# A hybrid attention block on one core: the causal mask added by TensorE, and a norm weight loaded as one row

## The chip, the core and the metric

The kernel runs on one core of a Trainium2 chip. The core has five engines that run side by side and wait for each other through semaphores: TensorE (PE in the profile; its weight loads are shown apart as PEld), VectorE (DVE), ScalarE (ACT), GpSimd (POOL) and SyncE (SP), which here issues all the transfers between HBM and the on-chip memory. Products are written to PSUM, which has 8 banks of 128 partitions by 512 fp32 numbers. The metric is the time of one execution on the device in microseconds (us), lower is better.

## What is computed

One layer of a streaming encoder on 1024 positions of width 1024, all in fp32:

```python
h = rms_norm(x, norm_pre_g)
proj = h @ w_in                          # -> sb_q, sb_k, sb_v, sb_g, c_q, c_kv, k_rope, mla_g
# group A: 8 stick-breaking heads; past = key < query (strictly)
log_fail = where(past, log_sigmoid(-z), 0); suffix = cumsum from the right
w = where(past, exp(log_sigmoid(z) + suffix), 0);  sb_o = w @ v
# group B: 8 latent-attention heads, chunk mask, softmax
y = concat(norm(sb_o) * silu(sb_g), norm(mla_o) * silu(mla_g)) @ w_out
x = x + rms_norm(y, norm_post_g)
x = x + rms_norm(p @ w_ple) * sigmoid(x @ w_ple_gate + b)
```

## The kernel before, in words

**Recorder and scheduler.** The program is not issued as it is written. A recorder takes down every operation, and a list scheduler (`schedule`, line 313) then decides the order on each engine from a table of costs and latencies, a priority per operation (its place in the code plus a bias, `R.bias`) and the buffers that are free. `issue` (line 482) issues the operations in that order; for that reason every row of the profile has the line L514. Tile names in rows: `u` and `f` are two pools of 512 KB buffers in SBUF, `t` are five PSUM banks (transposes and scores), `a` three PSUM banks (products that accumulate), `h` four large SBUF buffers (first the normed input, later the output weights), `ident` the identity for transposes.

**Precision.** For the large products every fp32 operand is split into a high part, which TensorE multiplies in one pass (type fp32r), and a low remainder (`split`: a cast, on ACT or DVE, and a subtraction, on DVE or POOL as the table `SPLITS` says); three products of the parts replace one. Transposes are products with the identity in fp32.

**Head.** `HEAD` orders the first transfers: a quarter of the v weights (`v0`), token tiles 1 and 0 of x, the vector norm_pre_g (`g0`), then the other quarters and x tiles. The vector is loaded by a transfer that reads its 4 KB 128 times and writes 512 KB, the same row on each partition (`bcast`, line 614). `x_norm` (line 639) squares a tile on ACT, takes the root on POOL and multiplies tile, root and vector in one DVE operation; `x_tr` (line 652) transposes the 128x1024 tile in two groups of four and splits the result; then the projections begin.

**Attention.** 16 head pairs (`SEQ`: head pair c, half s; c under 4 is stick-breaking, c from 4 on latent attention; s=0 is the first 512 queries, s=1 the second) are worked through one unit (one head, one half) after the other, in rows of 128 queries. `sb_rows` (line 1030) makes one stick-breaking row: two products into one or two PSUM banks, an addition of `maskt` (-1e30 on and above the diagonal) by DVE on the last 128 columns, two sigmoids by ACT, one product by POOL, one scan by DVE, one more product by POOL. `mla_rows` makes a latent row: three products, a DVE memset in place of a mask, row maxima by DVE, exponentials by ACT. `av` transposes the rows, splits them (ACT and DVE) and multiplies them with v. Between the rows, other work (projections, gates, low-rank products, output weights, first output tiles: `FILL0`, then `wo` and `e1`) is woven in; `RATES` says how much of it each unit takes.

**Tail.** After attention, `TAIL` orders the output products (`o`), the last gate products (`e`) and their loads (`x`) of the eight token tiles.

Of the kernel before, what the change touches and what calls it, by code (L numbers as in the profile page):

```python
# [12 lines left out]
F32 = mybir.dt.float32  # L13
F32R = mybir.dt.float32r
I32 = mybir.dt.int32
BF16 = mybir.dt.bfloat16
# [38 lines left out]
TAIL = ("x0", "o4", "o5", "o6", "x1", "x2", "e4", "o7", "e1", "x3", "e3", "e6", "e0", "e5", "e2", "e7")  # L55
RATES = (4.264, 8.284, 4.735, 4.524, 3.1, 1.429, 0.789, 1.173, 1.977, 0.816, 0.4, 1.023, 0.46, 0.671, 0.339, 1.676)
EARLY = 4
LATER = 5
SEQ = ((0, 0), (1, 0), (6, 0), (4, 0), (7, 0), (2, 0), (5, 0), (0, 1), (3, 0), (2, 1), (4, 1), (3, 1), (5, 1), (7, 1), (1, 1), (6, 1))
FILL0 = ("x4", "l0", "x5", "x6", "x7", "b1", "q1", "c0", "r3", "t0", "lrv0", "g3", "rope0", "r0", "g4", "r1", "q2", "r2", "q3", "g6", "g0", "g7", "g2", "g1", "ple0", "g5")  # L60
# [4 lines left out]
SPLITS = (1, 0, 1, 1, 0, 1, 1, 0, 1, 0, 1, 0, 1, 0, 0, 1, 1, 1, 1, 1, 1, 0, 1, 1, 1)  # L65
HEAD = ("v0", "x1", "x0", "g0", "v1", "v3", "v2", "x2")
# [93 lines left out]
class Recorder:  # L160
# [92 lines left out]
    def columns(self, op, args):  # L253

        return self.elems(args[0]) * (2 if op == "transpose" else 1 if args[1].dtype == F32R else 4)
# [8 lines left out]
    def cost(self, eng, op, args, kw, outs, aps, spaces):  # L264
        n = max(self.elems(a) for a in aps)
        ps = any(k == "psum" for _, k in spaces)
        if eng == "PE":
            n = self.elems(outs[0])
            if op == "transpose":
                return 109.0  # L270
            if aps[1].dtype == F32R:
                return n * 0.451 + 1 if n >= 256 else n * 1.67
# [244 lines left out]
def block_kernel(ctx, tc, x, p, positions, norm_pre_g, w_in, q_norm_g, w_uq, kv_norm_g, w_ukv,  # L517
# [44 lines left out]
    def small(tag, n=8, bufs=2):  # L562
# [5 lines left out]
    maskt = const([128, 128], "maskt")  # L568
    POOL.memset(maskt, 0.0)
    POOL.affine_select(maskt, maskt, pattern=[[-1, 128]], compare_op=ALU.is_gt, fill=NEG,  # L570
                       base=0, channel_multiplier=1)
    nhalf = const([128, 8], "nhalf")
# [66 lines left out]
    def x_norm(t):  # L639
# [6 lines left out]
        if t < EARLY:  # L646
            DVE.scalar_tensor_tensor(xt, xt, rs, gb["pre"], ALU.mult, ALU.mult)
# [67 lines left out]
    def first(item):  # L715
# [3 lines left out]
        elif k == "g":  # L719
            gb["pre"] = bcast(k4(dt=F32, name="gb_pre"), norm_pre_g, D)  # L720
# [35 lines left out]

    for item in HEAD:
        first(item)
    x_norm(0)
    x_norm(1)  # L760
    x_tr(0)
# [268 lines left out]
    def sb_rows(i, s, rows):  # L1030
        qa, qb, kk = stacks.pop((i, s))
        for qi in range(4):
# [5 lines left out]
            for ps, ks in tiles:  # L1038
                h = ks.stop - ks.start
                kw = slice(ks.start, ks.start + w)  # L1040
                mm(ps[:, 0:w], qa[:, qc], kk[:, kw], start=True, stop=False)
                mm(ps[:, 0:w], qb[:, qc], kk[:, kw], start=False, stop=True)
                if ks.stop == nk:
                    DVE.tensor_tensor(ps[:, h - 128:h], ps[:, h - 128:h], maskt, ALU.add)
# [377 lines left out]
```

## Time and profile before

| what | value |
|---|---|
| median of 3 runs (lowest to highest) | 795.59 us (793.53 to 798.85) |
| the profiled execution: its own time, its span | 796.6 us, 794.8 us |
| TensorE busy | 760.2 us (96%), 3880 products |
| VectorE busy | 544.2 us (68%) |
| ScalarE busy | 406.0 us (51%) |
| GpSimd busy | 344.1 us (43%) |
| share of the 16 transfer engines | 53.5% |

How to read it: busy time is the union of an engine's instructions. Products are pipelined and their ends are modelled, so short waits lie hidden in a busy TensorE. The program's own time is longer than the span by 1.8 us, which lie outside the instructions.

### The profile page before, as it was taken

The page shows a single profiled execution, that of the slowest core. Times are in us where ns is not written, and L with a number is a line of the kernel's source. Part 1 is how long each engine was busy: PE and PEld are TensorE (multiplying, and loading weights), DVE is VectorE, ACT ScalarE, POOL GpSimd, SP SyncE. Part 2 cuts the span into 40 slices and gives each one's busy share as a digit, 9 for nine tenths or more (in the row PEclk, how much of TensorE's full clock was granted, in tenths as well). Part 3 has the DMA queues.
Part 4 walks back from the last instruction along what each step waited for, and adds up shares of the span by engine and source line. Part 5 has one row for each costly group of instructions (what it writes and reads, how often), then busy time and mean ns, then how long its engine had stood idle before and what let it go on. Part 6 is the DMA issues. An engine that isn't in the chain of part 4 may idle for free. (4 is left out here: it accounts for less than half of the span.)

```text
span 794.8 us, 11668 instructions
## 1 busy us (share of the span) xinstructions
PE 760.2 (96%) x3880; PEld 629.5 (79%) x3880; DVE 544.2 (68%) x1063; ACT 406.0 (51%) x968; POOL 344.1 (43%) x321
## 2 busy tenths in 40 slices
PE   4999999999999999999998988999999999999997
PEld 3888889977888888788786767788888888788885
DVE  6866234399747796898788899999678897222222
ACT  5315123344436776766477878677966721121211
POOL 1836104102512270977980387233583183034342
PEclk9999999999999999999999999999999999999999
DMA  9554353187998576346754555867464364041321
GB/s 338 198 186 152 106 182 88 53 307 258 324 321 273 186 229 196 120 147 211 227 158 133 198 173 166 324 236 269 130 209 177 107 240 171 0 133 68 107 92 54
DMA packets 97308, 143.97 MB, mean 181 GB/s; under 512 B 7264, under 2 KB 54880, under 8 KB 97248
## 3 DMA queue, kind: packets, MB, share of 16 engines
q1 hardware_dynamic: 97248, 143.23, 53.5%
q8 instruction: 31, 0.51, 0.3%
q14 instruction: 29, 0.24, 0.1%
HBM read 96.54 MB, written 46.66 MB: 180 GB/s over the span
## 5 line engine op out<-in xcount | busy, mean ns | idle before, releaser
L514 POOL TENSOR_TENSOR u<-u,u 128x512 f32<-128x512 f32 (+17 forms) x168 | 234.9, 1411 | 202.9 <-ACT u L514 153.0
L514 PE MATMUL a<-h,f 128*128 128x512 f32 x864 | 238.1, 406 | 0.1
L514 PE MATMUL a<-u,u 128*128 128x512 f32 (+2 forms) x765 | 191.6, 377 | 0.3 <-DVE f L514 0.2
L514 PEld LDWEIGHTS a<-h,f 128*128 128x128 f32 x864 | 155.8, 189 | 28.7 <-DVE f L514 0.6
L514 DVE TENSOR_TENSOR u<-t,u 128x512 fp32r<-128x512 f32 (+4 forms) x280 | 147.2, 554 | 31.9 <-ACT u L514 25.3
L514 ACT CAST u<-t 128x512 fp32r<-128x512 f32 (+3 forms) x256 | 111.7, 488 | 97.7 <-PE t L514 74.5
L514 PEld LDWEIGHTS a<-u,u 128*128 128x128 f32 x765 | 138.1, 188 | 27.6 <-DVE u L514 0.9
L514 PE MATMUL t<-u,u 128*128 128x512 f32 (+4 forms) x588 | 147.5, 365 | 7.9 <-DVE u L514 4.6
L514 PE MATMUL t<-ident,u 128*128 128x128 f32 x792 | 131.5, 277 | 16.5 <-DVE u L514 13.5
L514 PEld LDWEIGHTS t<-u,u 128*128 128x128 f32 x588 | 101.5, 188 | 34.8 <-DVE u L514 10.3
L514 PEld LDWEIGHTS t<-ident,u 128*128 128x128 f32 x792 | 98.0, 142 | 37.1 <-DVE u L514 16.7
L514 ACT ACTIVATE u<-t 128x384 f32<-128x384 f32 (+5 forms) x208 | 92.7, 520 | 38.2 <-DVE t L514 22.2
L514 DVE TENSOR_TENSOR u<-a,u 64x512 f32<-64x512 f32 (+4 forms) x59 | 37.3, 641 | 75.4 <-PE a L514 63.4
L514 DVE TENSOR_TENSOR_SCAN u<-u 128x64 f32<-128x64 f32 (+3 forms) x64 | 63.8, 999 | 13.4 <-ACT u L514 13.0
L514 PE MATMUL a<-h,u 128*128 128x512 f32 x288 | 68.4, 396 | 1.4 <-DVE f L514 1.4
L514 ACT ACTIVATE f<-a 128x512 bf16<-128x512 f32 (+2 forms) x64 | 34.4, 539 | 67.2 <-PE a L514 52.6
L514 ACT ACTIVATE u<-t,nms 128x384 f32<-128x384 f32 (+4 forms) x96 | 55.1, 579 | 23.8 <-DVE nms L514 21.5
L514 PEld LDWEIGHTS a<-h,u 128*128 128x128 f32 x288 | 53.9, 188 | 14.5 <-DVE f L514 1.8
L514 DVE TENSOR_TENSOR f<-a,f 128x512 f32<-128x512 f32 (+2 forms) x54 | 34.4, 644 | 42.5 <-ACT f L514 41.1
L514 DVE TENSOR_REDUCE nm<-t 128x1 f32<-128x384 f32 (+4 forms) x96 | 51.9, 547 | 3.7 <-PE t L514 2.9
L514 PE MATMUL a<-u,h 128*128 128x512 f32 x192 | 49.1, 405 | 0.8 <-DVE h L514 0.8
L514 ACT ACTIVATE u<-u 128x512 f32<-128x512 f32 (+3 forms) x24 | 17.5, 739 | 51.6 <-DVE u L514 47.1
(90 smaller groups left out, 693.9 us busy)
## 6 DMA issues: line engine op xcount, KB each, us to landing
u<-q_d SPq DMA_DIRECT2D x64, 256.0 KB, 4.4
u<-k_d SPq DMA_DIRECT2D x16, 512.0 KB, 6.0
u<-v_d SPq DMA_DIRECT2D x16, 512.0 KB, 5.2
f<-in_w_in_dram SPq DMA_DIRECT2D x14, 512.0 KB, 5.7
v_d<-u SPq DMA_DIRECT2D x12, 512.0 KB, 3.9
f<-in_x_dram SPq DMA_DIRECT2D x9, 512.0 KB, 6.3
k_d<-u SPq DMA_DIRECT2D x9, 512.0 KB, 4.6
q_d<-u SPq DMA_DIRECT2D x9, 512.0 KB, 4.7
```

Source lines behind the costliest of these rows:

```text
L514: x["fn"](*[place(a) for a in x["args"]], **{k: place(a) for k, a in x["kw"].items()})
```

## The change

There are three edits and a new set of tables.

1. **The mask.** `maskt` becomes `mask`, of type bf16, and a bf16 identity `eye` is made beside it. The DVE addition goes; between a row's two score products stands a third that multiplies `eye` with `mask` and accumulates into the last 128 columns.
2. **The norm vector.** It is loaded as one row of 4 KB into one partition; two TensorE products with a row of ones spread each half of it over the 128 partitions, and two ACT copies bring it from PSUM to SBUF. These and the norm and transposes of tile 0 get priority (`URGENT`).
3. **Tile 0's norm** is made in two halves on DVE instead of one operation.
4. **Tables.** `SEQ`, `FILL0`, `RATES`, `SPLITS`, `TAIL` and `HEAD` have other entries.

```diff
-SEQ = ((0, 0), (1, 0), (6, 0), (4, 0), (7, 0), (2, 0), (5, 0), (0, 1), (3, 0), (2, 1), (4, 1), (3, 1), (5, 1), (7, 1), (1, 1), (6, 1))
+SEQ = ((0, 0), (1, 0), (6, 0), (4, 0), (7, 0), (2, 0), (0, 1), (3, 0), (3, 1), (2, 1), (5, 0), (5, 1), (7, 1), (4, 1), (1, 1), (6, 1))
-HEAD = ("v0", "x1", "x0", "g0", "v1", "v3", "v2", "x2")
+HEAD = ("v0", "x1", "x0", "g0", "v3", "v1", "v2", "x2")
+URGENT = 35
...
-    maskt = const([128, 128], "maskt")
-    POOL.memset(maskt, 0.0)
-    POOL.affine_select(maskt, maskt, pattern=[[-1, 128]], compare_op=ALU.is_gt, fill=NEG,
+    mask, eye = const([128, 128], "mask", BF16), const([128, 128], "eye", BF16)
+    POOL.memset(mask, 0.0)
+    POOL.affine_select(mask, mask, pattern=[[-1, 128]], compare_op=ALU.is_gt, fill=NEG,
                        base=0, channel_multiplier=1)
+    DVE.tensor_copy(eye, ident)
+    ones = const([1, 128], "ones")
+    POOL.memset(ones, 1.0)
...
         if t < EARLY:
-            DVE.scalar_tensor_tensor(xt, xt, rs, gb["pre"], ALU.mult, ALU.mult)
+            for v in half if t == 0 else [slice(0, D)]:
+                DVE.scalar_tensor_tensor(xt[:, v], xt[:, v], rs, gb["pre"][:, v], ALU.mult, ALU.mult)
...
-            gb["pre"] = bcast(k4(dt=F32, name="gb_pre"), norm_pre_g, D)
+            gb["pre"] = k4(dt=F32, name="gb_pre")
+            gb["row"] = k4(dt=F32, name="gb_row")
+            SP.dma_start(gb["row"][0:1], norm_pre_g[0:1, :])
...
+    R.bias = -URGENT
+    for n in range(2):
+        ps = ps_t()
+        mm(ps, ones, gb["row"][0:1, half[n]], start=True, stop=True)
+        ACT.copy(gb["pre"][:, half[n]], ps)
     x_norm(0)
+    x_tr(0)
+    R.bias = 0
     x_norm(1)
-    x_tr(0)
...
                 mm(ps[:, 0:w], qa[:, qc], kk[:, kw], start=True, stop=False)
+                if ks.stop == nk:
+                    mm(ps[:, h - 128:h], eye, mask, start=False, stop=False)
                 mm(ps[:, 0:w], qb[:, qc], kk[:, kw], start=False, stop=True)
-                if ks.stop == nk:
-                    DVE.tensor_tensor(ps[:, h - 128:h], ps[:, h - 128:h], maskt, ALU.add)
```

How the scheduler places this is seen in the order of the instructions. First TensorE at the start of the program, where `u_119` is token tile 1, `u_121` tile 0, `u_135`, `u_141`, `u_181`, `u_193` high and low parts of weight quarters, `h_0` and `h_2` high and low parts of the normed input. Before:

```order
L514 MATMUL t_174<-ident,u_119 128x128 x4
L514 MATMUL t_179<-ident,u_119 128x128 x2
L514 MATMUL t_186<-ident,u_121 128x128 x4
L514 MATMUL t_195<-ident,u_121 128x128 x4
L514 MATMUL t_179<-ident,u_119 128x128 x2
L514 MATMUL a_208<-u_135,h_0_183 128x512
L514 MATMUL a_208<-u_141,h_0_183 128x512
L514 MATMUL a_212<-u_135,h_0_183 128x512
L514 MATMUL a_212<-u_141,h_0_183 128x512
L514 MATMUL a_208<-u_135,h_2_220 128x512
```

Of the change, at the same place (`u_127` is the row, `u_125` tile 0, `u_139` and `u_145` parts of the first weight quarter):

```order
L517 MATMUL t_164<-u_127,ones 128x512
L517 MATMUL t_180<-u_127,ones 128x512
L517 MATMUL t_191<-ident,u_125 128x128 x4
L517 MATMUL t_198<-ident,u_125 128x128 x4
L517 MATMUL a_214<-u_139,h_0_202 128x512
L517 MATMUL a_214<-u_145,h_0_202 128x512
L517 MATMUL a_214<-u_139,h_2_220 128x512
```

Two products with the row stand ahead, and one tile is transposed instead of two before the projections begin.

VectorE over the same stretch. Before:

```order
L514 CAST u_135<-u_112 128x1024
L514 TENSOR_TENSOR u_141<-u_112,u_135 128x1024
L514 TENSOR_SCALAR sm_152<-ss_148 128x1
L514 TENSOR_SCALAR sm_166<-ss_158 128x1
L514 SCALAR_TENSOR_TENSOR u_119<-u_119,sr_156,u_123 128x1024
L514 SCALAR_TENSOR_TENSOR u_121<-u_121,sr_168,u_123 128x1024
L514 CAST u_181<-u_125 128x1024
L514 CAST u_189<-u_127 128x1024
L514 TENSOR_TENSOR u_193<-u_125,u_181 128x1024
L514 TENSOR_TENSOR u_206<-u_127,u_189 128x1024
L514 CAST u_215<-u_129 128x1024
L514 TENSOR_TENSOR h_2_220<-t_186,h_0_183 128x4x128
```

Of the change:

```order
L517 CAST u_139<-u_115 128x1024
L517 TENSOR_SCALAR sm_156<-ss_151 128x1
L517 TENSOR_SCALAR sm_172<-ss_160 128x1
L517 CAST u_178<-u_129 128x1024
L517 TENSOR_TENSOR u_186<-u_129,u_178 128x1024
L517 SCALAR_TENSOR_TENSOR u_125<-u_125,sr_174,u_183 128x512 x2
L517 CAST u_194<-u_131 128x1024
L517 CAST u_200<-u_133 128x1024
L517 TENSOR_TENSOR u_207<-u_131,u_194 128x1024
L517 TENSOR_TENSOR h_2_220<-t_191,h_0_202 128x4x128
```

The split of a second weight quarter moved ahead of tile 0's norm, two low parts of weight quarters went to POOL, and the norm of the other tile moved behind the first low part of the input (`h_2`), on which the third projection product waits.

The first stick-breaking rows on TensorE, where `t_186` and its like are score banks. Before:

```order
L514 MATMUL t_186<-u_454,u_545 128x256
L514 MATMUL t_179<-u_454,u_545 128x256
L514 MATMUL t_270<-u_454,u_545 128x384
L514 MATMUL t_195<-u_454,u_545 128x512
L514 MATMUL t_174<-ident,u_143 128x128 x2
```

Of the change:

```order
L517 MATMUL t_180<-u_470,u_558 128x256
L517 LDWEIGHTS eye
L517 MATMUL t_180<-mask,eye 128x128
L517 MATMUL t_198<-u_470,u_558 128x512
L517 MATMUL t_191<-u_470,u_558 128x256
```

Each row has one more weight load and one product of 128 columns; there are 64 of each in the program.

Three counts from the two orders, of places that the tables move. ACT loads a function table 26 times before and 18 times now, since stick-breaking and latent units alternate less. The transposes of TensorE stand in 270 runs between other products before and in 246 now (880 transposes in both). The eight low parts of the output weights (`wo_gen`, line 1216) were made by DVE and POOL, four each; now DVE makes all eight. They stand in both orders in the same part of the program, among the units of latent heads with s=1, and in the change four latent pairs follow each other there, (5, 0), (5, 1), (7, 1) and (4, 1), where before the stick-breaking pair (3, 1) stood among them.

## Rows read from the trace of the kernel before

**Rows 1.** The page: busy time, share of the span and instructions of each engine

```profile
PE 760.2 (96%) x3880; PEld 629.5 (79%) x3880; DVE 544.2 (68%) x1063; ACT 406.0 (51%) x968; POOL 344.1 (43%) x321
```

**Rows 2.** The timeline, 0 to 40 us: start, duration, engine, operation, count, idle before

```profile
1.24 0.93 SPq L514 DMA_DIRECT2D u<-in_x_dram  x2
...
9.34 2.48 DVE L514 SCALAR_TENSOR_TENSOR u<-u,sr,u 128x1024 f32<-128x1024 f32 x2 [0.46 <-DMA u<-in_norm_pre_g_dram]
...
10.68 3.68 PE L514 MATMUL t<-ident,u 128*128 128x128 f32 x16 [10.68 <-DVE u L514]
11.74 1.29 DVE L514 CAST u<-u 128x1024 fp32r<-128x1024 f32 x2
...
12.94 2.35 DVE L514 TENSOR_TENSOR u<-u,u 128x1024 fp32r<-128x1024 f32 x2
13.12 0.59 ACT L514 CAST h<-t 128x512 fp32r<-128x512 f32 x1 [0.69 <-PE t L514]
...
14.01 1.72 PE L514 MATMUL a<-u,h 128*128 128x512 f32 x4
...
15.82 0.68 DVE L514 TENSOR_TENSOR h<-t,h 128x512 fp32r<-128x512 f32 x1
...
16.56 5.38 PE L514 MATMUL a<-u,h 128*128 128x512 f32 x22 [0.82 <-DVE h L514]
...
21.77 1.03 PE L514 MATMUL t<-ident,u 128*128 128x128 f32 x8
```

**Rows 3.** The second of these x transfers (1.7 to 2.0 us): size, us to landing

```profile
u<-in_x_dram SPq DMA_DIRECT2D x1, 512.0 KB, 5.8
```

**Rows 4.** The timeline of TensorE, 690 to 745 us

```profile
718.66 11.39 PE L514 MATMUL a<-u,u 128*128 128x512 f32 x48
```

**Rows 5.** The timeline of TensorE, 357.0 to 357.5 us

```profile
357.02 0.39 PE L514 MATMUL a<-u,u 128*128 128x512 f32 x1
357.25 0.27 PE L514 MATMUL t<-ident,u 128*128 128x128 f32 x1
357.27 0.48 PE L514 MATMUL a<-u,u 128*128 128x512 f32 x1
```

**Rows 6.** Groups of instructions by form: count, busy us, mean ns

```profile
L514 PEld LDWEIGHTS t<-ident,u 128*128 128x128 f32 x792 | 98.0, 142 | 37.1 <-DVE u L514 16.7 <-ACT u L514 6.7 <-POOL u L514 0.7
...
L514 ACT ACT_TABLE_LOAD x26 | 33.4, 1283 | 6.6 <-DVE nms L514 5.4 <-PEq L1403 0.7
...
L514 POOL TENSOR_TENSOR h<-f,h 128x1024 fp32r<-128x1024 f32 x4 | 10.5, 2613 | 16.5 <-DVE h L514 16.5
...
L514 DVE TENSOR_TENSOR h<-f,h 128x1024 fp32r<-128x1024 f32 x4 | 5.8, 1443 | 0.0
```

**Rows 7.** The mask tile: its instructions, then who waited for it (us, times)

```profile
L514 DVE TENSOR_TENSOR t<-t,maskt x64: 260/289/300, 61.8 to 592.5; 128x128 f32<-128x128 f32 x64
...
  ACT u L514: 22.2, 16
```

**Rows 8.** The mask tile, 400 to 500 us

```profile
L514 DVE TENSOR_TENSOR t<-t,maskt x10: 268/286/300, 402.7 to 485.2; 128x128 f32<-128x128 f32 x10
```

**Rows 9.** Waits of the weight loads on others: us in total, times, longest

```profile
PEld t L514 <- DVE u L514: 27.5, 34, 10.7
PEld t L514 <- ACT u L514: 14.6, 36, 1.5
```

**Rows 10.** Busy time in stretches: us, then each engine, clock, transfers

```profile
400.00:440.00 40.00, 37.58 (x207) 30.68 (x206) 35.64 (x68) 30.93 (x72) 17.93 (x17) 1.00 0.47 150
440.00:480.00 40.00, 35.81 (x196) 28.24 (x195) 34.76 (x71) 30.72 (x80) 23.48 (x19) 1.00 0.50 167
480.00:520.00 40.00, 36.40 (x206) 30.50 (x205) 37.54 (x78) 29.90 (x72) 22.10 (x18) 1.00 0.76 257
```

**Rows 11.** Busy time in one late stretch: the same columns

```profile
690.00:790.00 100.00, 99.45 (x455) 81.04 (x453) 25.46 (x39) 19.29 (x34) 36.59 (x29) 1.00 0.26 87
```

More of the change, by code (lines that the diff above doesn't have):

```diff
@@ L54 @@
 TICK = 10240.0 / 3.0
-TAIL = ("x0", "o4", "o5", "o6", "x1", "x2", "e4", "o7", "e1", "x3", "e3", "e6", "e0", "e5", "e2", "e7")
-RATES = (4.264, 8.284, 4.735, 4.524, 3.1, 1.429, 0.789, 1.173, 1.977, 0.816, 0.4, 1.023, 0.46, 0.671, 0.339, 1.676)
+TAIL = ("x1", "o4", "o5", "o6", "x2", "x3", "o7", "e3", "x0", "e4", "e0", "e1", "e5", "e2", "e6", "e7")
+RATES = (4.934, 9.256, 4.735, 4.518, 3.1, 1.436, 0.789, 0.703, 2.078, 0.654, 0.4, 0.788, 0.251, 0.582, 0.808, 2.854)
+URGENT = 35
 EARLY = 4
 LATER = 5
-SEQ = ((0, 0), (1, 0), (6, 0), (4, 0), (7, 0), (2, 0), (5, 0), (0, 1), (3, 0), (2, 1), (4, 1), (3, 1), (5, 1), (7, 1), (1, 1), (6, 1))
-FILL0 = ("x4", "l0", "x5", "x6", "x7", "b1", "q1", "c0", "r3", "t0", "lrv0", "g3", "rope0", "r0", "g4", "r1", "q2", "r2", "q3", "g6", "g0", "g7", "g2", "g1", "ple0", "g5")
+SEQ = ((0, 0), (1, 0), (6, 0), (4, 0), (7, 0), (2, 0), (0, 1), (3, 0), (3, 1), (2, 1), (5, 0), (5, 1), (7, 1), (4, 1), (1, 1), (6, 1))
+FILL0 = ("x4", "x5", "l0", "x6", "x7", "q1", "c0", "b1", "r3", "t0", "lrv0", "g3", "rope0", "r0", "g4", "r1", "q2", "r2", "q3", "g0", "g6", "g1", "g2", "g7", "ple0", "g5")
 N1 = 3
@@ L64 @@
 LOWS = ("g", "q", "ple", "x", "b", "c", "t", "l")
-SPLITS = (1, 0, 1, 1, 0, 1, 1, 0, 1, 0, 1, 0, 1, 0, 0, 1, 1, 1, 1, 1, 1, 0, 1, 1, 1)
-HEAD = ("v0", "x1", "x0", "g0", "v1", "v3", "v2", "x2")
+SPLITS = (1, 0, 0, 1, 0, 1, 1, 1, 1, 1, 1, 1, 0, 0, 0, 1, 1, 0, 0, 0, 1, 0, 1, 1, 0)
+HEAD = ("v0", "x1", "x0", "g0", "v3", "v1", "v2", "x2")
 AHEAD = 52
@@ L253, in columns @@
     def columns(self, op, args):
-        return self.elems(args[0]) * (2 if op == "transpose" else 1 if args[1].dtype == F32R else 4)
+        return self.elems(args[0]) * (2 if op == "transpose" else 1 if args[1].dtype in (F32R, BF16) else 4)
     @staticmethod
@@ L270, in cost @@
                 return 109.0
+            if aps[1].dtype == BF16:
+                return max(60.0, n * 0.451)
             if aps[1].dtype == F32R:
```

## The prediction

> **What bounds it now.** I read the page first. TensorE is busy 760.2 of 794.8 us, VectorE 544.2, the others less [rows 1]: TensorE is the bound, and 34.6 us of it are idle. Of these 10.7 lie before its first instruction and 0.8 before the projections run through [rows 2]. Next I read busy time in stretches. The tail is dense: 99.45 of 100 us between 690 and 790, with VectorE at a quarter [rows 11]. Attention is not: between 400 and 520 us TensorE is busy 109.8 of 120 us and VectorE 107.9 [rows 10]; 10.2 us are idle, and there VectorE is as much the bound as TensorE. Last I read the waits of the weight loads, which show more than the waits of the products, since those hide short waits in modelled ends: 27.5 us on VectorE, of which 10.7 is the head, so 16.8 later, and 14.6 on ScalarE in 36 places [rows 9]. So the change can gain in the head and in these 31 us, and it pays with work on the engine that bounds.
>
> **The head.** VectorE waited for the vector until 9.34 us [rows 2]. Two tiles of x are issued in 0.93 us from 1.24 on; the second one, issued near 1.7, lands 5.8 us later, at 7.5 [rows 2, 3]. So the vector held the queue for some 1.8 us. No row shows a transfer of 4 KB; it lands between 7.5 and 9.3, and I take 7.6, behind the tile. Then come two plain fp32 products of 512 columns, which the trace does not have. Below, the split products of that width took 1.72/4 = 0.43 each here; an fp32 transpose of 128 columns took 3.68/16 = 0.23, four of them 0.92 [rows 2]. I take 0.92, since that row has the type, and twice that as the upper end. With 0.2 for the handover and 0.59 for a copy by ScalarE [rows 2] the first half stands in SBUF at 9.3, the second at 10.2.
>
> But VectorE is not free then. Its order now has the split of the next weight quarter ahead of the norm. That quarter follows the tile in the queue, where 512 KB took some 1.3 us, so it lands at 8.9; cast and subtraction (1.29/2 = 0.65, 2.35/2 = 1.18 [rows 2]) end at 10.7. The two halves of the norm, 0.62 each (half of 2.48/2), end at 11.3 and 12.0. The first transposes begin at 11.4 instead of 10.68. Two casts and a subtraction follow (2.5), then the first low part of the input (0.68 [rows 2]): 15.2. Before, that part ended at 15.82 + 0.68 = 16.5, and the projections ran on from 16.56. So they run on 1.3 us earlier, with eight transposes (1.03 [rows 2]) and two products (2 x 0.24, from 5.38/22 [rows 2]) less behind them. The two cancel within 0.2. With products of 1.84 the second half comes at 12.1 and costs another 0.5. **Head: +0.3**, between -1.3 (the eight transposes find a gap) and +1.7 (the copies also delay the squares on ScalarE). The wait that is removed is real, but VectorE's splits stand in its place.
>
> **Mask products.** 64 products of 128 columns are added, each with a weight load. A product of 512 columns alone comes every 11.39/48 = 0.237 us [rows 4]; with one 128-column product between, two of them stand 357.27 - 357.02 = 0.25 apart [rows 5]. So a lone short product between wide ones costs as little as 0.013. At most it costs a whole weight load, 0.142 [rows 6], and its columns, a quarter of 0.237: 0.20. The mask stands alone between two products of 256 to 512 columns, which is the first case; it is of another type, so I leave some room and take 0.045: **+2.9**, between +0.8 and +12.8.
>
> The Trainium skill ("TensorE: Matmul & The Clock Gate", "Back-to-back issue gap") gives a sustained spacing of about 81 ns for products of 128 columns, because the weight load takes part in it; by that the term would be +5.2. The trace agrees where short products follow each other (1.03/8 = 0.13 us) and not where one stands alone (0.25 against 0.237).
>
> **Transposes in fewer runs.** 24 short runs are gone. A transpose inside a run costs 1.03/8 = 0.13 [rows 2], a lone one 0.013 to 0.06; 24 x 0.08 = **+1.9**, between 0 and +2.8.
>
> **What the chain gets back.** The mask addition took 0.287 us each, 64 times, and ScalarE waited 22.2 us for it in 16 places [rows 7]. ScalarE is busy half the time [rows 1], so this wait alone is worth nothing; it counts where the score banks then come free late, and that is the wait of weight loads for ScalarE, 14.6 us [rows 9]. Stick-breaking rows make about half of the rows, and their chain gets shorter by 0.3 and two handovers; I take a third, 4.9. Of the 16.8 us on VectorE I take the share of its work that goes, 64 x 0.287 = 18.4 of 544 us [rows 1, 7], 3% or 0.6. **-5.5**, between 0 and the whole of what waits on both, -31.
>
> **The stretch that VectorE bounds.** Between 400 and 500 us stand 10 of the additions [rows 8]: 10 x 0.286 = 2.9 us less. But four low parts of the output weights come to VectorE from GpSimd, 4 x 1.443 = 5.8 [rows 6], and they stand in the same run of latent units. Net +2.9 for VectorE. It is busy 89 to 94% there and TensorE 90 to 94% [rows 10], so about half shows: **+1.5**, between -2.9 and +5.8.
>
> **Table loads.** 8 loads fewer at 1.283 us [rows 6] are 10.3 us for ScalarE. It has slack beside TensorE, busy 29.9 to 30.9 of 40 us in the tightest stretches [rows 10], which hides most; without that cover each costs what a wait on ScalarE costs, 14.6/36 = 0.4, or 3.2 in all. **-1.0**, between 0 and -3.2.
>
> **The other tables** (`TAIL`, `FILL0`, `HEAD`, the mask as a constant, `eye`) order the same work anew; the tail has 0.5% idle to win [rows 11], and I take 0.
>
> **The sum.** 0.3 + 2.9 + 1.9 - 5.5 + 1.5 - 1.0 = +0.1. The profiled execution took 796.6 us, 1.0 above the median of the runs, so it becomes 796.7, and a median of 795.7.
>
> **The rivals.**
> - *The chain gives back much more.* If the 16.8 us that TensorE waits on VectorE in attention vanish with the additions, in place of the 5.5, the sum is 0.3 + 2.9 + 1.9 - 16.8 + 1.5 - 1.0 = -11.2, or 784. For it: VectorE is the last releaser in the stretch with most idle time [rows 9, 10]. Against it: only 10 of the additions are there [rows 8], and VectorE gets the output weights.
> - *The mask's weights are not hidden.* TensorE must load `eye` and then the second query half, with 128 columns between to cover a load of 0.142. At 0.20 each, 12.8 in place of 2.9, the sum is +10.0, or 805.6. It decides from 0.19 us per mask product on. For it: in runs of short products the load shows. Against it: the lone transpose [rows 5].
> - *The latent pairs in a row choke on VectorE.* TensorE's idle share there is 10.2 of 120 us [rows 10]; if it doubles over some 110 us, that is +9, or 804.7.
>
> **Chances.** The forecast, within its own range of 789 to 802, has 0.60; the first rival 0.25; the two others 0.15 together. About 1%, 8 us, is what a measurement of this kernel can tell from no change. Faster by over 1% means under 787.6: the first rival, 0.25. Slower means over 803.5: 0.15. Within 1%: 0.60. The range of 8 in 10 reaches half into the rivals at either end: 783 to 804.5.
>
> **What would show it.** The head is right if TensorE's first projections run through near 15 us and its first product with the row stands near 7.6; it is wrong if transposes begin before 10.7. The mask term is right if score products with a mask between them stand no more than 0.1 us further apart than two without. The chain is right if weight loads wait some 9 us on ScalarE instead of 14.6. The stretch is right if, among the four latent pairs, VectorE is above 90% and TensorE below 95%. I would be wrong most likely in the waits: if TensorE's idle time in attention falls below 5 us, the first rival holds.

## The result, and the profile after

The changed kernel takes 791.48 us (median of 12 runs, 788.54 to 793.85); the kernel before, run beside it, 796.02 (12 runs, 793.53 to 799.00). The ratio is 0.9938 with a 95% interval of 0.9919 to 0.9957: faster by 0.6%. That is inside the range on record (783.0 to 804.5) and inside the forecast's own range (789 to 802), but it is not the "no change" of the forecast: the interval excludes 1. The profiled execution of the changed kernel took 793.85 us, the slowest of the twelve, with a span of 792.1. That lies 2.4 us above its median, the profiled execution of the kernel before 0.6 us above its own, so a difference between the two traces can be off by some 2 us.

The page, busy time, share of the span and instructions of each engine, against [rows 1]:

```profile
PE 768.9 (97%) x3948; PEld 634.2 (80%) x3948; DVE 537.6 (68%) x1006; ACT 394.6 (50%) x961; POOL 330.1 (42%) x318
```

TensorE is busy 8.7 us longer in a span that is 2.7 us shorter. So its busy time grew (the products with the row alone are 3.75 us of it, below), and about 11 us of idle time went.

The head, from the timeline of the changed kernel (start, duration, engine, operation, count, idle before), against [rows 2]:

```profile
7.22 3.75 PE L517 MATMUL t<-u,ones 1*128 1x512 f32 x4 [7.22 <-DMA u<-in_norm_pre_g_dram]
...
9.30 0.59 ACT L517 COPY u<-t 128x512 f32<-128x512 f32 x1 [0.91 <-PE t L517]
9.32 1.23 DVE L517 TENSOR_TENSOR u<-u,u 128x1024 fp32r<-128x1024 f32 x1
...
10.46 0.75 DVE L517 SCALAR_TENSOR_TENSOR u<-u,sr,u 128x512 f32<-128x512 f32 x1
...
11.26 2.28 PE L517 MATMUL t<-ident,u 128*128 128x128 f32 x8 [0.30 <-DVE u L517]
...
14.63 1.28 DVE L517 TENSOR_TENSOR h<-t,h 128x512 fp32r<-128x512 f32 x2
...
15.37 5.17 PE L517 MATMUL a<-u,h 128*128 128x512 f32 x13 [0.97 <-DVE h L517]
...
20.38 1.03 PE L517 MATMUL t<-ident,u 128*128 128x128 f32 x8
```

The row is there at 7.22, and the projections run through from 15.37, 1.2 us earlier than before. But 13 of them take until 20.38: 0.39 us each, where 22 took 5.38 us before, 0.24 each [rows 2]. The trace's record of the granted clock has its first entry, the rise to the full level, at 19.6 us here and at 15.2 before. (Ahead of the first entry the record is empty, and the stretches of the profile show 1.00 there; the spacing of the products shows that it was the lower level.) The changed kernel has 24 transposes and 24 projection products behind it at 24.14 us (20.38 + 0.79 + 9 products + eight more transposes). Before, 24 transposes and 26 products were done at about 22.6 (21.77 and 0.8 for eight transposes [rows 2]), so the same work some 2 us earlier.

Attention, busy time in the three stretches of [rows 10] (us; PE, PEld, DVE, ACT, POOL busy; clock; transfers):

```profile
400.00:440.00 40.00, 37.64 (x196) 30.04 (x195) 32.25 (x45) 27.59 (x66) 28.30 (x24) 1.00 0.47 155
440.00:480.00 40.00, 39.21 (x223) 32.69 (x222) 37.38 (x99) 28.31 (x79) 14.75 (x17) 1.00 0.78 253
480.00:520.00 40.00, 39.09 (x219) 32.18 (x218) 38.04 (x84) 29.76 (x74) 4.24 (x7) 1.00 0.79 264
```

TensorE is busy 115.9 of 120 us; 4.1 us are idle, where 10.2 were. VectorE is busy as long as before (107.7 against 107.9).

The waits of the weight loads and products of the score banks on others (us in total, times, longest), against [rows 9]:

```profile
PEld t L517 <- DVE u L517: 7.3, 18, 1.9
...
PEld t L517 <- ACT u L517: 6.7, 21, 1.4
...
PEld t L517 <- DMA u<-q_d: 5.2, 3, 2.2
...
PE t L517 <- DMA u<-q_d: 4.2, 3, 1.9
```

Weight loads wait 7.3 us on VectorE, 2.3 of them in the head (before 27.5, of which 10.7 were the head), and 6.7 on ScalarE (before 14.6). A wait has become larger: 5.2 us on the transfers that bring the queries back from HBM (`q_d`), where the kernel before has

```profile
PEld t L514 <- DMA u<-q_d: 2.0, 2, 1.3
```

The chain of work that ended last goes through them (start, us, what):

```profile
55.42 3.05 DMA q_d<-u
58.47 0.02 issue
58.49 1.35 SPq L517
59.84 0.04 issue
59.88 5.79 DMA u<-q_d
...
107.34 5.30 DMA q_d<-f
...
113.05 5.35 DMA u<-q_d
...
118.44 1.73 PE t L517 x5
120.17 10.68 PE a L517 x52
```

Behind the second one TensorE's granted clock falls to its lower level; the first of these two stretches holds the wait, the second the fall (0.57 is a mean of both levels):

```profile
112.00:118.00 6.00, 3.81 (x20) 2.74 (x18) 0.69 (x1) 1.37 (x2) 1.96 (x1) 1.00 0.62 150
118.00:122.00 4.00, 3.56 (x11) 3.18 (x12) 2.22 (x4) 2.75 (x8) 2.40 (x5) 0.57 0.75 275
```

### The profile page after: what moved, and what is told of

It is laid out like the page before. It is cut to its first block, busy times and chain, and to the rows that moved or that the text cites. A ratio compares the mean times of both kernels' runs of the same rounds, so it can differ in the third digit from the quotient of the medians.

```text
span 792.1 us, 11714 instructions
## 1 busy us (share of the span) xinstructions
PE 768.9 (97%) x3948; PEld 634.2 (80%) x3948; DVE 537.6 (68%) x1006; ACT 394.6 (50%) x961; POOL 330.1 (42%) x318
## 4 chain that ended last, share of the span: by engine, by line
PE 86%; DMA 6%; DVE 5%; ACT 2%; issue 1%; SPq 1%; DVEq 0%; ACTq 0%
PE a L517 61%; PE t L517 24%; DVE u L517 2%; DVE f L517 1%; ACT u L517 1%; DMA u<-q_d 1%; DMA f<-in_w_in_dram 1%; DMA y_d<-u 1%; DVE nm L517 1%; DMA q_d<-f 1%; SPq L517 1%; DMA u<-in_norm_pre_g_dram 1%; DMA k_d<-f 1%; ACT f L517 0%; DMA q_d<-u 0%
## 5 line engine op out<-in xcount | busy, mean ns | idle before, releaser
L517 POOL TENSOR_TENSOR u<-u,u 128x512 f32<-128x512 f32 (+17 forms) x155 | 216.1, 1405 | 165.6 <-ACT u L517 81.9
L517 PE MATMUL a<-u,u 128*128 128x512 f32 (+2 forms) x762 | 188.4, 378 | 1.3 <-DVE u L517 0.6
L517 DVE TENSOR_TENSOR u<-t,u 128x512 fp32r<-128x512 f32 (+4 forms) x280 | 146.4, 554 | 25.2 <-ACT u L517 23.4
L517 ACT CAST u<-t 128x512 fp32r<-128x512 f32 (+3 forms) x256 | 113.4, 492 | 94.9 <-PE t L517 79.0
L517 PE MATMUL t<-u,u 128*128 128x512 f32 (+4 forms) x576 | 152.4, 370 | 4.5 <-DMA u<-q_d 4.2
L517 PE MATMUL t<-ident,u 128*128 128x128 f32 x792 | 126.5, 275 | 2.4 <-ACT u L517 1.7
L517 ACT ACTIVATE u<-t 128x384 f32<-128x384 f32 (+5 forms) x208 | 91.1, 518 | 46.3 <-PE t L517 35.0
L517 DVE TENSOR_TENSOR_SCAN u<-u 128x64 f32<-128x64 f32 (+3 forms) x64 | 69.4, 1094 | 27.4 <-ACT u L517 24.4
L517 POOL MEMSET u<- 128x128 f32 x64 | 12.5, 208 | 106.0 <-PE t L517 38.2
L517 PE MATMUL a<-u,h 128*128 128x512 f32 x192 | 51.7, 417 | 1.0 <-DVE h L517 1.0
```

The costliest lines, as they stand in the source:

```text
L517: x["fn"](*[place(a) for a in x["args"]], **{k: place(a) for k, a in x["kw"].items()})
```

## The experiments

Three theories were weighed. One: the edits work as the prediction's terms say, each with a price of its own, so parts done alone should add up. Two: the scheduler decides the whole order anew at any edit, the tables fit one order, and what is measured is mostly the order. Three: the head loses time because TensorE's clock is late, and the loss hides part of a larger gain. There are two kinds of runs. In the first eight, and in the three that move one number (e16 to e18), the scheduler makes the order anew. In the kernels named "hold" the order that the scheduler gives stays, instruction for instruction on every engine, and only the disputed instructions are left out at the moment of issue or ride ahead of another one.

| run | order | vector | mask by | us | ratio to before, interval |
|---|---|---|---|---|---|
| changed kernel | its own | row | TensorE | 791.48 | 0.9938 (0.9919 to 0.9957) |
| e1_mask | old tables, anew | 512 KB | TensorE | 808.15 | 1.0145 (1.0123 to 1.0167) |
| e2_head | old tables, anew | row | VectorE | 805.33 | 1.0108 (1.0084 to 1.0132) |
| e3_tables | new tables, anew | 512 KB | VectorE | 797.91 | 1.0017 (1.0001 to 1.0033) |
| e4_mask_tables | new tables, anew | 512 KB | TensorE | 793.55 | 0.9961 (0.9943 to 0.9979) |
| e5_head_tables | new tables, anew | row | VectorE | 801.63 | 1.0069 (1.0043 to 1.0096) |
| e6_mask_head | old tables, anew | row | TensorE | 809.28 | 1.0168 (1.0142 to 1.0193) |
| e7_warm_after | new tables, anew | row, 24 transposes ahead | TensorE | 787.37 | 0.9886 (0.9865 to 0.9907) |
| e8_mask_twice | new tables, anew | row | TensorE, twice | 801.14 | 1.0058 (1.0038 to 1.0079) |
| e9_hold_mask | before's, held | 512 KB | TensorE | 799.22 | 1.0046 (1.0028 to 1.0065) |
| e10_hold_add | changed, held | row | VectorE, misplaced | 804.63 | 1.0113 (1.0094 to 1.0132) |
| e11_hold_bcast | changed, held | 512 KB | TensorE | 788.37 | 0.9914 (0.9895 to 0.9934) |
| e12_hold_warm | changed, held | row, 24 transposes ahead | TensorE | 787.87 | 0.9898 (0.9879 to 0.9918) |
| e13_hold_add2 | changed, held | row | VectorE | 803.33 | 1.0091 (1.0075 to 1.0108) |
| e14_hold_row | before's, held | row | VectorE | 799.28 | 1.0039 (1.0025 to 1.0054) |
| e15_hold_warm2 | changed, held | row, 40 transposes | TensorE | 783.92 | 0.9851 (0.9832 to 0.9870) |
| e16_null_before2 | before, one number moved | 512 KB | VectorE | 804.24 | 1.0111 (1.0086 to 1.0135) |
| e17_null_before | before, one number moved | 512 KB | VectorE | 806.96 | 1.0114 (1.0080 to 1.0147) |
| e18_null_after2 | changed, one number moved | row | TensorE | 797.32 | 0.9998 (0.9983 to 1.0014) |

### The parts alone and in pairs

`e1_mask` has the mask on TensorE with the old tables, `e2_head` the row, its products and copies and the halved norm with the old tables, `e3_tables` the new tables alone; the other three leave one of the parts away.

```diff
 # e1_mask, on the kernel before
+                if ks.stop == nk:
+                    mm(ps[:, h - 128:h], eye, mask, start=False, stop=False)
-                    DVE.tensor_tensor(ps[:, h - 128:h], ps[:, h - 128:h], maskt, ALU.add)
 # e2_head, on the kernel before
-            gb["pre"] = bcast(k4(dt=F32, name="gb_pre"), norm_pre_g, D)
+            gb["pre"] = k4(dt=F32, name="gb_pre")
+            gb["row"] = k4(dt=F32, name="gb_row")
+            SP.dma_start(gb["row"][0:1], norm_pre_g[0:1, :])
 # e3_tables, on the kernel before: all six tables, as
-HEAD = ("v0", "x1", "x0", "g0", "v1", "v3", "v2", "x2")
+HEAD = ("v0", "x1", "x0", "g0", "v3", "v1", "v2", "x2")
```

> The kernel before with the mask as a product of TensorE alone: old tables, old loading of the norm vector. Theory A (the waits): the gain comes from the additions that leave VectorE, whose queue releases the score banks and rows late; then this alone gives most of the 0.6%, a ratio of 0.990 to 0.996. Theory B (the tables): the gain comes from the other order of units; then this alone pays 64 products at 0.04 us, 2.6 us, and gets little back: 1.000 to 1.004.

> The kernel before with the norm vector loaded as a row and spread by TensorE, tile 0's norm in halves, its priority; mask and tables as before. Theory C (the clock and VectorE's splits eat the gain): the projections run through at about the same place but with fewer transposes done and at twice the spacing for longer, so it costs 1 to 3 us: 1.001 to 1.004. If the removed wait were a gain, 0.997 to 0.999.

> The kernel before with only the tables of the change (unit order, filling, rates, splits, tail, head order). Theory B: most of the gain is here, 0.990 to 0.996, and TensorE's idle time between 380 and 520 us falls from 11.7 us to under 7. Theory A: 0.998 to 1.004, with the idle time about as before.

> The change without its head: mask on TensorE and new tables, but the norm vector is again spread by the transfer. Theory C: the head costs 1 to 3 us in the change, so this is faster than the change, 0.990 to 0.993 against the kernel before. If the head is a gain in the change: 0.995 to 0.998.

> The change without its mask product: VectorE adds the mask again; new head and tables. Theory A: the gain is gone, 0.999 to 1.004. Theory B: 64 products at 0.04 us are saved and little is lost, 0.990 to 0.994.

> The change with the tables of the kernel before: mask product and head alone. Theory A: 0.992 to 0.997. Theory B: 1.002 to 1.006.

Measured: 808.15, 805.33, 797.91, 793.55, 801.63 and 809.28 us. The parts do not add up: 1.45%, 1.08% and 0.17% slower alone, 0.6% faster together. The mask costs 1.45% with the old tables; with the new ones it gains 0.6% (e3 to e4), and 1.3% beside the row (e5 to the changed kernel). Either the edits depend on the tables in their mechanism, or any order that the old tables give anew is a poor one. These six do not tell these apart; e16 and e17 do. As expectations they mostly missed: e1, e2, e5 and e6 came out slower than every case on record. e3 fits the case in which the tables alone gain nothing. e4 came out where the head would be a gain in the change, against e11 below; the two differ in their order, and an order alone is worth 0.6% here (e18), so e4 decides nothing.

### An edit that does nothing

```diff
 # e16 on the kernel before, e18 on the changed one; in e17 AHEAD = 53
-LOW = 336
+LOW = 337
```

> The kernel before with the planner's number LOW at 337 in place of 336: the same instructions of the same kinds, in an order made anew. Theory S (the planner's tables fit one order, and any other costs): 1.005 to 1.015, 800 to 808 us, with the loss between 380 and 540 us, as in e1, e2 and e6. Theory T (the order made anew costs nothing; the edits did): 0.998 to 1.003.

> The kernel before with the planner's number AHEAD at 53 in place of 52: a second order made anew, with the same work. Theory S (the planner's tables fit one order, and any other costs): 1.005 to 1.015, 800 to 808 us. Theory T (the order made anew costs nothing; the edits did): 0.998 to 1.003.

> The changed kernel with the planner's number LOW at 337 in place of 336. Theory S (its tables too fit one order): 0.999 to 1.010 against the kernel before, 795 to 804 us. Theory T (the changed work is easier to order, so another order does as well): 0.991 to 0.997, 789 to 794 us.

Measured: 804.24, 806.96 and 797.32 us. The same work as before, ordered anew, is 1.1% slower, twice; the changed work, ordered anew by a number moved by one, is 0.6% slower than in its own order and level with the kernel before. The last of the three stretches of attention, of e16 and then of e17, beside 36.40 us of TensorE and a clock of 1.00 before [rows 10]:

```profile
480.00:520.00 40.00, 33.28 (x167) 27.51 (x166) 35.02 (x71) 24.58 (x60) 19.38 (x17) 0.87 0.67 228
```

```profile
480.00:520.00 40.00, 33.89 (x183) 27.02 (x183) 32.44 (x71) 26.38 (x68) 17.83 (x17) 1.00 0.66 227
```

So e2's 1.0108 is no more than these two idle edits cost with the old tables, and e1's 1.0145 and e6's 1.0168 lie only 0.3 and 0.6% above them. "The mask costs 12 us" would have been a false reading of e1. What an edit costs has to be seen with the order held.

### The mask with the order held

```diff
 # e9_hold_mask, on the kernel before: the product rides ahead, the addition is left out
+    R.ins[-1]["ahead"] = [(nc.tensor.matmul, (ps[:, h - 128:h], eye, mask), dict(start=False, stop=False))]
     DVE.tensor_tensor(ps[:, h - 128:h], ps[:, h - 128:h], maskt, ALU.add)
+    R.ins[-1]["skip"] = True
 # e13_hold_add2, on the changed kernel: the other way round
     mm(ps[:, h - 128:h], eye, mask, start=False, stop=False)
+    R.ins[-1]["skip"] = True
+                add = {"todo": [(nc.vector.tensor_tensor, (ps[:, h - 128:h], ps[:, h - 128:h], maskt, ALU.add), {})]
+                       if ks.stop == nk else ()}
                 ACT.activation(u[:, ks], ps[:, 0:h], AF.Sigmoid, scale=-SB_SCALE)
+                R.ins[-1]["first"] = add
                 ACT.activation(row[:, ks], ps[:, 0:h], AF.Sigmoid, scale=SB_SCALE)
+                R.ins[-1]["first"] = add
```

> The kernel before, instruction for instruction in its own order on every engine, with one exchange: the 64 additions of the mask on VectorE are left out and the 64 mask products ride directly ahead of the second score product of the same bank. So nothing is rescheduled. Theory M (the exchange itself brings the gain: VectorE's step leaves the chain from scores to sigmoid): +2.9 us for the products, about -7.7 us of TensorE's idle time between 380 and 520 us, so 791 us, ratio 0.994. Theory O (the exchange costs its products and little comes back while the order stays; the gain of the change is in its order): 796 to 799 us, ratio 1.000 to 1.004. If the old order with the exchange were the cause of the 1.0145 of e1_mask: 807 us; then the freshly made order is not what hurt there.

> The counterpart: the changed kernel in its own order on every engine, with the 64 mask products left out and an addition by VectorE directly ahead of the first sigmoid of each bank in their place. Theory M: the products' 2.9 us go, the wait on VectorE comes back in the stretch from 380 to 520 us, 791.5 - 2.9 + 7.7 = 796 us, ratio 1.001. Theory O: the new order bears the additions about as well, 791.5 - 2.9 + (0 to 3) = 788.6 to 791.6 us, ratio 0.9905 to 0.9945. The idle time of TensorE from 380 to 520 us decides besides the time: near 12 us by M, near 4 us by O.

> The changed kernel in its own order, the mask products left out, the 64 additions on VectorE put back, each ahead of whichever of the bank's two sigmoids is issued first. (In e10_hold_add the addition stood ahead of one fixed sigmoid; where the other is issued first, that one read scores without the mask, and VectorE waited for it: that run's time is not a time of this exchange.) Theory M (the new order is good only because the additions are gone): 796 us or more, ratio 1.000 or more, and TensorE idle some 8 us or more from 380 to 520 us. Theory O (the order is the gain, with or without additions): 788.6 to 791.6 us, ratio 0.9905 to 0.9945, idle near 4 us there.

e9 took 799.22 us, 3.6 more than before: the low case. The 64 products cost their time and next to nothing of the total comes back. Weight loads wait less on ScalarE (8.5 us for 14.6) and on VectorE (22.9 for 27.5), but TensorE still idles 8.4 us from 400 to 520 us (10.2 before), and in this execution its clock falls there once:

```profile
PEld t L517 <- DVE u L517: 22.9, 26, 10.5
PEld t L517 <- ACT u L517: 8.5, 24, 1.3
```

```profile
480.00:520.00 40.00, 37.53 (x205) 31.42 (x205) 37.24 (x75) 29.71 (x71) 22.18 (x18) 0.96 0.74 254
```

In e10 the addition stood ahead of one fixed sigmoid; where the scheduler issues the other one first, that one read scores without the mask and the addition waited for it, so its 804.63 us is not a time of this exchange. e13 mends that, and took 803.33 us, 11.9 more than the changed kernel in the same order: beyond the high case. The waits of e13 (us, times, longest):

```profile
ACT u L522 <- DVE t L519: 37.2, 37, 3.6
...
PEld t L522 <- ACT u L522: 24.1, 51, 2.4
...
PEld t L522 <- DVE u L522: 7.7, 18, 1.8
```

ScalarE waits 37.2 us for the additions, and weight loads 24.1 us for ScalarE, where the changed kernel has 6.7. Their wait for VectorE itself hardly differs (7.7 against 7.3): in this order the additions cost through ScalarE, which has to wait for them. The idle time is not where it was expected. From 400 to 520 us TensorE idles 4.8 us in e13 and 4.1 in the changed kernel; the difference lies on both sides of that, first two stretches of e13, then the same two of the changed kernel:

```profile
240.00:380.00 140.00, 136.00 (x738) 111.10 (x737) 111.16 (x228) 92.07 (x219) 89.57 (x89) 1.00 0.56 181
520.00:690.00 170.00, 165.67 (x874) 136.89 (x872) 133.80 (x257) 97.15 (x231) 54.11 (x50) 1.00 0.52 174
```

```profile
240.00:380.00 140.00, 139.13 (x787) 114.99 (x786) 114.17 (x204) 92.42 (x222) 91.23 (x92) 1.00 0.58 185
520.00:690.00 170.00, 169.88 (x895) 141.34 (x895) 131.04 (x246) 95.55 (x229) 53.58 (x50) 1.00 0.52 171
```

TensorE idles 4.0 and 4.3 us there with the additions, 0.9 and 0.1 without. So the exchange is worth -11.9 us in the changed kernel's order and +3.6 in that of before. The 11.9 overstate it: an order that is made with the additions in mind, from the same tables (e5), does better than e13 by 1.7 us; and before's own order, the best with additions of all these runs, does better by 7.7.

### The mask product twice

```diff
                     mm(ps[:, h - 128:h], eye, mask, start=False, stop=False)
+                    mm(ps[:, h - 128:h], eye, mask, start=False, stop=False)
```

> The change with the mask product made twice in each row (twice -1e30 on the masked columns). It prices the product alone: if a lone product of 128 columns costs its 0.04 us on the engine that bounds, 64 more cost 2.6 to 4 us, 0.997 to 0.999 against the kernel before; if the weight load shows, 64 at 0.2 cost 12.8 us, 1.009 or more.

Measured 801.14 us, 9.7 more than the changed kernel. By itself this is not a price of the product, since the order is made anew; beside e18, the changed work in another new order, it is 3.8 us, 0.06 each (4.8 by the two ratios). It lies between the two cases on record and decides neither. The trace of the changed kernel shows the price directly (timeline of TensorE):

```profile
440.34 0.40 PE L517 MATMUL t<-u,u 128*128 128x512 f32 x1
440.58 0.23 PE L517 MATMUL t<-mask,eye 128*128 128x128 bf16 x1
440.62 0.48 PE L517 MATMUL t<-u,u 128*128 128x512 f32 x1
```

The two score products stand 0.28 us apart, where a 512-column product alone comes every 0.237 [rows 4]: 0.04 us for the mask between them, 2.8 us for 64. The place is typical: over the whole trace the median is 0.277 us for the 11 such pairs and 0.232 for the 155 pairs of 512 columns without a mask.

### The head with the order held

```diff
 # e7_warm_after, on the changed kernel, among the first transfers: the order is made anew
+    for _ in range(6):
+        ps = ps_t()
+        for a in range(4):
+            PE.transpose(ps[:, a * 128:(a + 1) * 128], ident, ident)
 # e14_hold_row, on the kernel before: the row in place of the 512 KB, two products and two copies ahead of the norm
+            R.ins[-1]["behind"] = [(nc.sync.dma_start, (gb["pre"][0:1], norm_pre_g[0:1, :]), {})]
+    scale["ahead"] = [r for n in range(2) for r in (
+        (nc.tensor.matmul, (trp[n], ones, gb["pre"][0:1, half[n]]), dict(start=True, stop=True)),
+        (nc.scalar.copy, (gb["pre"][:, half[n]], trp[n]), {}))]
 # e11_hold_bcast, on the changed kernel: the other way round
+            R.ins[-1]["behind"] = [(nc.sync.dma_start, (gb["pre"], norm_pre_g[0:1, :].broadcast_to([128, D])), {})]
 # e12_hold_warm, on the changed kernel, ahead of the first product with ones; e15_hold_warm2: 26, and 14 ahead of the first transpose of x
+            R.ins[-1]["ahead"] = [(nc.tensor.transpose, (ps[:, 0:128], ident, ident), {})] * 24
```

> The kernel before in its own order, with the vector loaded as a row of 4 KB and spread by the two products with ones (into the banks of the first transposes, ahead of them) and two copies by ScalarE; nothing else moves. e2_head, the same with an order made anew from the old tables, took 1.0108. Theory S (those 8.6 us were the remade order): within 3 us of before, 795 to 799 us, ratio 0.998 to 1.004; the upper part if the late full clock costs 2 to 3 us as e11 and e12 say of the changed kernel. Theory T (the row itself costs): 803 us or more, ratio 1.008 or more.

> The changed kernel in its own order, with the head's vector loaded again as 128 rows by one transfer, and the two products with ones and the two copies left out. Theory H1 (the row shortens the head, as its first projections at 15.37 against 16.56 us say): 0.5 to 1.2 us more than the changed kernel, 792.0 to 792.7, ratio 0.9945 to 0.9955. Theory H2 (the row's products and copies and the full clock that comes only at 19.6 us lose 2 us, and nothing later makes it good): 789.5 us, ratio 0.992. Theory H3 (a loss in the first 25 us is made good by the first waits behind it): the same time as the changed kernel within 0.3 us, ratio 0.994.

> The change with 24 transposes of the identity put ahead of its first product with the row, in the time in which TensorE waits for the first transfers (1.5 to 7 us); their results are not used. Theory C: the spacing of the first projection products, 0.43 us between 15.4 and 19.4 us in the change, falls to about 0.23 there, because TensorE was active earlier, and the time falls by 2 us or so: a ratio to the kernel before of 0.989 to 0.993. If the clock does not matter in the head: as the change, 0.9938.

> The changed kernel in its own order, with 24 transposes of the identity into the bank of the first product with ones, ahead of it, so that TensorE works from about 5 us on. e7_warm_after had 24 such transposes too but in an order of its own, and took 787.4 us, 4.1 less than the changed kernel. Theory C (the clock that comes late in the head is the cause; the projections at 15.4 us then run at the granted full clock, 0.23 in place of 0.43 us each, some 2 us earlier from there on): 789 to 790 us, ratio 0.9915 to 0.993. Theory R (e7's gain came from another order, the clock of 4 us is absorbed by a later wait): 791 to 792 us, ratio 0.994.

> The changed kernel in its own order, with 26 transposes of the identity ahead of the first product with ones and 14 more between the second and the first transposes of x, so that TensorE hardly idles between 1.5 and 11.5 us. e12 (24 ahead, then 2.2 us idle) took 787.9 us, and its clock was at half level from 7.9 to 14.7 us. Theory C (the clock in the head is worth its time one for one): the first 24 projection products and their transposes are done at 22.1 in place of 23.8 us, so 786 us, ratio 0.988. Theory R (some lead at 25 us is enough, the rest is lost in a later wait for a transfer): as e12, 787.5 to 788, ratio 0.990.

Measured: e14 799.28 us, 3.7 more than before; e11 788.37, 3.1 less than the changed kernel. By the ratios to the kernel that ran beside each, e11's lead is only 0.24%, 1.9 us, and the two intervals overlap (0.9895 to 0.9934, 0.9919 to 0.9957). So in the order of before the row costs 3 to 4 us; in that of the change it costs 2 to 3, not clear of the noise, and of that only 0.7 lies in the head (e11 has 24 transposes and 24 products done at 23.4 us, the changed kernel at 24.1). Nowhere is it faster than the transfer that it replaces. In e14's timeline:

```profile
6.92 3.75 PE L515 MATMUL t<-u,ones 1*128 1x512 f32 x4 [6.92 <-DMA u<-in_norm_pre_g_dram]
12.72 3.67 PE L517 MATMUL t<-ident,u 128*128 128x128 f32 x16 [2.05 <-DVE u L517]
...
18.59 5.37 PE L517 MATMUL a<-u,h 128*128 128x512 f32 x22 [0.49 <-DVE h L517]
```

The first transposes come 2.0 us later than before (10.68), and the projections run through 2.0 us later (16.56) [rows 2]. The two products took 1.87 us each, and the norm, whole here, waits for both. That is 2.0 of the 3.7 us; the projections themselves run at the full clock here (0.24 us each), so the rest lies behind them.

e7, with 24 transposes in banks of their own and so in an order made anew, took 787.37 us, 4.1 less than the changed kernel; that this is no luck of its order is shown by e12, the same with the order held, at 787.87.

e12 also shows the changed kernel's late clock. Its projections, in the timeline, and the stretch around them:

```profile
15.10 5.08 PE L520 MATMUL a<-u,h 128*128 128x512 f32 x13 [0.59 <-DVE h L520]
```

```profile
15.00:19.00 4.00, 3.90 (x9) 3.13 (x10) 3.46 (x7) 2.88 (x6) 2.78 (x4) 0.50 1.07 348
```

Thirteen products in 5.08 us, as in the changed kernel, and here the row has the granted clock: 0.50, the lower of the two levels, 1.2 GHz. e12 had worked for 4.74 us at the start, in which the record shows the full level from 5.4 us on, and then stood idle twice, for 0.98 us ahead of the row's products and 2.17 us behind them; the record shows the lower level from 8.8 to 19.1 us. (The text on record for e15 gives e12 the stretch from 7.9 to 14.7 us; that is e7's.) e15 fills these gaps; its stretch:

```profile
15.00:19.00 4.00, 4.00 (x24) 3.31 (x22) 2.72 (x7) 4.00 (x10) 2.51 (x4) 1.00 1.07 346
```

24 products in the 4 us, eight of them transposes, where e12 has 9. e15 took 783.92 us (783.67 to 784.49), 7.5 less than the changed kernel and 1.5% less than the kernel before: the fastest kernel here, faster than both. The expectation was 786, so more came back than the head itself. The chain of e15 shows where; two pieces of it:

```profile
35.09 16.77 PE a L520 x72
...
112.09 9.83 PE a L520 x52
```

The 72 products begin at 37.27 in the changed kernel, 2.2 us later: that is the head. The 52 products begin at 120.17 there (above), 8.1 us later, and take 0.85 us longer with the fallen clock. Between them lie the two round trips of `q_d`, for which TensorE waits in the changed kernel and not in e15. e12 has only 0.3 us of lead at 24 us and still ends at 787.87; in its trace most of the wait for `q_d` is missing too (1.4 us for 5.2). So the head itself is 2.2 us, and the rest of the 7.5 depends on what the round trips do. (The changed kernel's trace is that of its slowest execution, 2.4 us above the median, so part of the 8.1 is that execution.) Why they took longer in the changed kernel is open: one issue of a read took 1.35 us and a write took 5.30 us to land there, 0.54 and 3.13 in e12, and there is one trace of each kernel.

The late clock is not settled by the order of the head alone. On TensorE e5 and e6 begin with the same products in the same order as the changed kernel, the first 200 and more, and have no extra transposes; e5:

```profile
7.21 3.75 PE L517 MATMUL t<-u,ones 1*128 1x512 f32 x4 [7.21 <-DMA u<-in_norm_pre_g_dram]
...
15.35 3.28 PE L517 MATMUL a<-u,h 128*128 128x512 f32 x13 [0.76 <-DVE h L517]
```

The thirteen products take 3.28 us instead of 5.17, in e6 too, and the record has the full clock from 15.0 and 14.1 us on. Of the nine traces with the row and without extra transposes, these two have it at 14.1 to 15.0 us and seven at 18.6 to 21.2; the eight with the 512 KB transfer have it at 13.8 to 16.1. e5's six times fall into two groups, 799.1 to 799.8 and 803.4 to 804.2 us, and its trace is of the first. That the clock of the head divides them is likely but not shown, with one trace of each kernel.

## Why the prediction was wrong

**The bound, and where to look.** Right: TensorE is the bound, the idle time of attention and the waits of the weight loads are where the gain came from.

**The head, +0.3.** Wrong for the execution that was traced: 24 transposes and 24 products are done some 2 us later than before. By e11 the row costs 3.1 us (1.9 by the ratios, not clear of the noise). e14's 3.7 has another cause, since there the whole norm waits for both products. The steps held to their end: the row at 7.22 (forecast 7.6), VectorE's split in place of the removed wait (9.32 to 10.55), transposes at 11.26 (11.4), the projections through at 15.37 (15.2). Two prices failed. The fp32 products took 3.75/2 = 1.87 us each, the upper end of the bounds, 0.92 had been taken; that cost little, since the split ended at 10.55. And the price of the products behind them was taken from before at 0.24 us; they ran at the lower clock, 0.39, for 13 products some 2 us. A late clock was not in the sum at all. Where the clock came early, the forecast was right: in e5 the 24 transposes and 24 products are done at 22.22 us, in the kernel before some 22.1.

**Mask products, +2.9.** Right: 0.04 us each in the rows, 2.8 us. The rival of weights that are not hidden is out (its border of 0.19 us per product should read 0.17: 2.9 and 7.8 us over 64). The Trainium skill ("TensorE: Matmul & The Clock Gate", "Back-to-back issue gap") would make it an estimated 5.2; the trace does not agree where the short product stands between two wide ones (0.04 us). Nor does it agree in the number where short ones follow each other: the prediction's 0.13 is for transposes in fp32, and above the 0.081 of the Trainium skill.

**Transposes in fewer runs, +1.9.** Not tested by itself; it lies inside what the order is worth.

**What the chain gives back, -5.5; the stretch that VectorE bounds, +1.5.** This is the step that failed on the other side. The weight loads' waits fell by more than was taken: on ScalarE to 6.7 us (forecast some 9), on VectorE behind the head from 16.8 to 5.0 (0.6 taken off). The stretch has VectorE at 94% from 440 to 520 us, as forecast, but TensorE at 98%, not below 95: VectorE's work there did not hold it up. The prediction priced the additions as a share of waits in the order of before. In that order the runs agree with its low bound: nothing came back in the time (e9). In the order of the changed kernel the exchange is worth 11.9 us (e13). It was no constant of the edit.

By the prediction's own sign the first rival holds, since 4.1 us of idle time are left. Its mechanism, waits on VectorE that vanish with the additions, is not what e13 shows: there the additions return and the waits on ScalarE grow. Its price, 784, was not reached either. e15 took 783.9 with a head about as early as that of before (24 transposes and 24 products at 21.95 us), but only 2.2 of its 7.5 us lie in the head and the rest is open, so this agreement is in part luck.

**Table loads, -1.0.** The count is right (18), the price was not tested.

**The other tables, 0.** About right alone (e3: +0.17%) and wrong in kind: the order decides whether the other terms come at all. The changed work with a number moved by one is level with before (e18).

**The sum.** Head +3.1 by e11 and mask products +2.8 leave -10.4 for everything else in the -4.5 measured; the prediction had -3.1 there. Two errors of opposite sign, 2.8 and 7.3 us (1.6 and 6.1 with the head at 1.9), left one of about 4.5 against the kernel before (4.2 in the time itself). So the larger error is in what the chain gives back, which no edit has by itself and the order decides. Why this order uses the exchange and that of before does not is shown as far as the waits go (24.1 us on ScalarE with the additions, 6.7 without) and open beyond that.

## What to carry to other kernels

Where a scheduler decides the order from tuned tables, an edit's first measurement is that of a new order: run an edit that does nothing beside it (here it cost 1.1% of the kernel before and 0.6% of the changed one), and price the edit with the order held. A gain at a wait is worth only what the order around it can use, so the same exchange can cost 3.6 us in one order and gain 11.9 in another (against additions put back into that order, an upper figure). In the head of a kernel, look at when TensorE's clock reaches its full level and not only at when the first product starts; 40 useless transposes, which kept TensorE at work while it waited, gave more than the whole change.

## What was not expected of the hardware

- A plain fp32 product of 512 columns with one row of weights took 1.87 us at the lower clock, recorded in two parts; the split product of the same width took 0.43 there. Where the full level was on record for most of that time (e12, up to 8.8 us), the two fp32 products together took 2.14 us instead of 3.75.
- An earlier start mostly went with a later full clock: TensorE began at 7.22 us (e14: 6.92), worked 3.75 us, paused, and had the full clock from 19.6 us on (e14: 18.6); before, it began at 10.68 and had it from 15.2 on. e5 and e6, which began at 7.21 and 7.01 with the same products, had it from 15.0 and 14.1 on, so this varies; what divides them is open.
- TensorE's clock also falls in a kernel that is 97% busy: behind a wait of 1.9 us for `q_d` at 118 us, and in e16 a stretch of 40 us with 6.7 us of idle time had a mean of 0.87. It need not fall: in e17 the same stretch with 6.1 us of idle time had 1.00.
- A bf16 product of 128 columns with weights of its own, between two 512-column products, costs 0.04 us.
